# The last dense block of a decoder-layer kernel finished in quarters of 256 columns instead of halves of 512

## The chip, the cores and the metric

The kernel runs on one core of a Trainium2 chip, as one launch. The metric is the device time of that launch in microseconds (us), the median of several executions; lower is better.

## The reference

One decoder layer on 512 tokens of width 1024: a mixer (sliding-window attention beside gated linear attention), then a retrieval of experts, then a final norm. Only the end matters here:

```
def peer_ffn(h, wq, subkeys, u, v):
    ...                                   # 16 experts per head and token, gates by softmax
        hid = jax.nn.gelu(jnp.einsum('tkd,td->tk', ub, xb), approximate=False) * gb
        return jnp.einsum('tk,tkd->td', hid, vb)
...
        x = x + gate2 * peer_ffn(h2, peer_wq[l], peer_subkeys[l], peer_u[l], peer_v[l])
    return rms_norm(x, final_norm_w)      # x * rsqrt(mean(x*x) + 1e-6) * w
```

There are 16384 experts, so `u` and `v` are 16384 x 1024 each, in float32.

## The kernel before

The 512 tokens are four blocks of 128. Blocks 0, 1, 2 (`DENSE`, called `n0`, `n1`, `n2` at the end) are computed densely: every expert's weight for every token stands in a matrix `A` that is mostly zeros, and the block's result is A^T times `v`. Block 3 (`GB`) gathers its experts' rows instead and is finished earlier.

The dense product runs over 128 chunks of 128 experts. Each operand is split into a high and a low part, and `mm3` issues three matmuls per product (lines 98, 99 and 100: high by high, high by low, low by high). The results gather in six accumulators of PSUM, `acc[2*i + q]` for block i and half q of the 1024 columns. Each accumulator has 128 x 512 float32 and fills one bank of PSUM. So `acc0` and `acc1` belong to block 0, `acc2` and `acc3` to block 1, `acc4` and `acc5` to block 2.

For most chunks all six accumulators are served in turn. The last four chunks (`LAST = 4`, the list `last`) are kept back and done block by block, so that block 0 is complete first: 24 matmuls into `acc0` and `acc1`, then 12 into `acc2`, 12 into `acc3`, 12 into `acc4` and 12 into `acc5`. These are the last matmuls of the program.

Then each block is closed. `close_half(n, src, q)` multiplies a half of the accumulator by the gate (L2041, VectorE), adds the residual (L2042, VectorE), and squares the result on ScalarE with a running sum (L2043, followed by a read of the sum, ACTIVATION_READ_ACCUMULATOR). `root(n)` adds the two half sums (L2048), scales them (L2049), and takes the reciprocal root through Ln and Exp on ScalarE (L2050, L2051). `refine(n)` is a correcting step on VectorE (L2057, L2058). `weighted(n, q, w)` multiplies a half by the norm's weights before the root is known (L2061, VectorE), and `scaled` finishes it with the root on ScalarE (L2064) and stores it from ScalarE's queue. `last_half` does both multiplications in one VectorE instruction (L2073) and stores from SP's queue.

Each engine executes its instructions in the order in which they stand in the program. Between engines, the framework places semaphore waits: an instruction waits for what wrote its operands. The two halves of block 2 are closed around the root of block 1, as the end of the printed code shows.

Of the kernel before, what the change touches and what calls it, by code (L numbers as in the profile page):

```python
# [7 lines left out]
F32 = mybir.dt.float32  # L8
# [4 lines left out]
AF = mybir.ActivationFunctionType  # L13
OP = mybir.AluOpType
# [3 lines left out]
P = 128  # L18
D = 1024
# [3 lines left out]
EPS = 1e-6  # L23
# [4 lines left out]
DENSE = (0, 1, 2)  # L28
# [41 lines left out]
def peer_block_kernel(ctx: ExitStack, tc: tile.TileContext, a: dict, out: bass.AP):  # L70
    nc = tc.nc
# [25 lines left out]
    def mm3(acc, lh, ll, rh, rl, start, stop):  # L97
        nc.tensor.matmul(acc, lh, rh, start=start, stop=False)  # L98
        nc.tensor.matmul(acc, lh, rl, start=False, stop=False)  # L99
        return nc.tensor.matmul(acc, ll, rh, start=False, stop=stop)  # L100
# [112 lines left out]
    for L in LW:  # L213
        m = 64 >> L
# [1666 lines left out]
    dn = ctx.enter_context(tc.tile_pool(name="dn", bufs=1, side="right", reuse_waits="tile"))  # L1881
    pacc = ctx.enter_context(tc.tile_pool(name="pacc", bufs=1, space=PSUM, side="right", reuse_waits="tile"))
    acc = [pacc.tile([P, 512], F32, name=f"acc{i}") for i in range(2 * len(DENSE))]
# [131 lines left out]
    def v_matmuls(parts, blocks=range(len(DENSE)), qs=(0, 1)):  # L2015
        for c, Ah, Al, vh, vl in parts:
            for i in blocks:
                for q in qs:
                    mm3(acc[2 * i + q], Ah[:, i * P:(i + 1) * P], Al[:, i * P:(i + 1) * P],
                        vh[:, q * 512:(q + 1) * 512], vl[:, q * 512:(q + 1) * 512], c == 0, c == P - 1)  # L2020
# [8 lines left out]
    def half(t, q):  # L2029
        return t[:, q * 512:(q + 1) * 512]  # L2030

    gate2b = h2n
    fin = {}
# [5 lines left out]
    def close_half(n, src, q):  # L2039
        y, xr, ss = fin[n][:3]  # L2040
        nc.vector.tensor_tensor(half(y, q), src, half(gate2b, q), OP.mult)  # L2041
        nc.vector.tensor_tensor(half(y, q), half(y, q), half(xr, q), OP.add)  # L2042
        nc.scalar.activation(half(xr, q), half(y, q), AF.Square, accum_out=ss[:, q:q + 1])  # L2043

    def root(n):
        ss = fin[n][2]
        m, r = ss[:, 2:3], ss[:, 3:4]
        nc.vector.tensor_tensor(ss[:, 0:1], ss[:, 0:1], ss[:, 1:2], OP.add)  # L2048
        nc.vector.tensor_scalar(m, ss[:, 0:1], -0.5 / D, -0.5 * EPS, op0=OP.mult, op1=OP.add)  # L2049
        nc.scalar.activation(r, m, AF.Ln, scale=-2.0)  # L2050
        nc.scalar.activation(r, r, AF.Exp, scale=-0.5)  # L2051
        fin[n] += [m, r]

    def refine(n):
        m, r = fin[n][3:5]
        t = fin[n][2][:, 4:5]
        nc.vector.scalar_tensor_tensor(t, r, r, m, op0=OP.mult, op1=OP.mult)  # L2057
        nc.vector.scalar_tensor_tensor(r, t, 1.5, r, op0=OP.add, op1=OP.mult)  # L2058

    def weighted(n, q, w):  # L2060
        nc.vector.tensor_tensor(half(w, q), half(fin[n][0], q), half(fin["w"], q), OP.mult)  # L2061

    def scaled(n, q, w):
        nc.scalar.activation(half(w, q), half(w, q), AF.Copy, scale=fin[n][4])  # L2064
        store(n, q, w, nc.scalar)

    def store(n, q, t, eng=None):
        (eng or nc.sync).dma_start(out[n * P:(n + 1) * P, q * 512:(q + 1) * 512], half(t, q))

    def last_half(n, qs=(1,)):  # L2070
        y, r = fin[n][0], fin[n][4]
        for q in qs:
            nc.vector.scalar_tensor_tensor(half(y, q), half(y, q), r, half(fin["w"], q), op0=OP.mult, op1=OP.mult)  # L2073
            store(n, q, y)
# [38 lines left out]
    for i in range(end):  # L2113
        k, c = xs[i]
# [16 lines left out]
    last = [part for i in range(end, len(xs)) for part in ready.pop(i)]  # L2131
    v_matmuls(last[:3], (0,))
    v_matmuls(last[3:], (0,))
    for b in DENSE[1:]:
        for q in range(2):
            v_matmuls(last, (b,), (q,))

    dn.tile([P, 32], F32, name="gap")
    n0, n1, n2 = DENSE
# [12 lines left out]
    close_half(n1, acc[3], 1)  # L2152
    weighted(n1, 0, w1)
    root(n1)
    close_half(n2, acc[4], 0)
    refine(n1)
    last_half(n1)
    scaled(n1, 0, w1)
    close_half(n2, acc[5], 1)
    weighted(n2, 0, w2)  # L2160
    root(n2)
    weighted(n2, 1, w2)
    refine(n2)
    scaled(n2, 0, w2)
# [64 lines left out]
```

## Time and profile before

| what | value |
|---|---|
| median of 3 runs | 1419.93 us (1419.32 to 1423.29) |
| the profiled execution | 1420.04 us, of which its span is 1418.1 us |
| busy: TensorE matmuls, VectorE, ScalarE | 98%, 89%, 46% of the span |
| last matmul starts | 1409.82 us after the span's start |
| last VectorE and ScalarE instructions start | 1414.00 us |

PE is TensorE, PEld its weight loads, DVE VectorE, ACT ScalarE, POOL GpSimd, SP SyncE; ACTq and SPq are those engines' queues of DMA issues. In a timeline row the columns are the start in us from the span's start, the duration in us, the engine, the line, the operation with its tiles (output, arrow, inputs; numbers of buffers are left out), its sizes, and how many instructions the row holds. In brackets stands how long the engine had been idle and what released it. A following instruction of the same engine may start a little before the former one's end, since the engines are pipelined.

### The profile page before, as it was taken

The numbers are of one execution on the slowest core, as the hardware profiler recorded it, in microseconds if no ns is written. First come the engines' busy times: TensorE is split into PE (matmuls) and PEld (weight loads), VectorE is DVE, ScalarE is ACT, GpSimd is POOL, SyncE is SP. The second block draws the span as 40 slices with busy tenths as digits, with TensorE's granted clock in tenths as the row PEclk, the third lists the DMA queues.
The fourth block names the chain that finished last, engine by engine and source line by source line (L and its number), as shares of the span: only waits on it lengthen the run. The fifth ranks groups of instructions, "written<-read, shape, count | busy, mean of one in ns | idle before, by whom it ended". The sixth has DMA issues, their size and how long they took to land.

```text
span 1418.1 us, 23363 instructions
## 1 busy us (share of the span) xinstructions
PE 1394.5 (98%) x8838; PEld 1226.5 (86%) x8838; DVE 1258.4 (89%) x2312; ACT 658.9 (46%) x1116; POOL 604.0 (43%) x397
## 2 busy tenths in 40 slices
PE   8999999999999999999989999999999999999997
PEld 5777788988999999999978888888888888888886
DVE  7768888679899999998969899989898998998996
ACT  4458565533534567667844333333333333333333
POOL 1000000344616443232045766767677776555520
PEclk9999999999999999999999999999999999999999
DMA  9621567422559989899889999999999999999972
GB/s 356 258 93 58 165 221 246 133 98 70 193 193 413 339 320 378 320 349 345 296 326 414 412 412 413 411 412 411 402 405 387 403 378 412 402 412 405 411 260 75
DMA packets 128305, 439.88 MB, mean 310 GB/s; under 512 B 11936, under 2 KB 48832, under 8 KB 107840
## 3 DMA queue, kind: packets, MB, share of 16 engines
q1 hardware_dynamic: 69600, 252.73, 47.2%
q0 software_dynamic: 47136, 171.99, 31.0%
q10 hardware_dynamic: 11456, 13.67, 2.7%
q8 instruction: 69, 1.13, 0.3%
q14 instruction: 44, 0.36, 0.1%
HBM read 395.78 MB, written 42.47 MB: 309 GB/s over the span
## 4 chain that ended last, share of the span: by engine, by line
PE 80%; DVE 7%; issue 6%; POOL 3%; DMA 2%; ACT 2%; SPq 0%; POOLq 0%; DVEq 0%; ACTq 0%
PE acc L98 12%; PE acc L100 12%; PE acc L99 12%; PE ph L98 8%; PE ph L100 8%; PE ph L99 8%; POOL spr L1631 3%; PE pq L99 2%; PE pq L98 2%; PE pq L100 2%; PE pg L1552 2%; PE pw L98 1%; PE pw L100 1%; PE pw L99 1%; PE pj L509 1%
## 5 line engine op out<-in xcount | busy, mean ns | idle before, releaser
L98 PE MATMUL ph<-h2Th,his 128*128 128x320 f32 x1024 | 319.5, 312 | 2.8 <-ACT his L1995 1.9
L100 PE MATMUL ph<-h2Th,los 128*128 128x320 f32 x1024 | 316.0, 310 | 2.5 <-DVE los L2002 1.8
L99 PE MATMUL ph<-h2Tl,his 128*128 128x320 f32 x1024 | 316.0, 309 | 0.0
L1687 POOL DMA_INDIRECT gu<-in_u_dram,ix_u x128 | 212.1, 1657 | 151.1 <-DVE gu L1697 82.4
L1722 POOL DMA_INDIRECT gv<-in_vP_dram,ix_v x128 | 210.2, 1642 | 111.9 <-DVE gacc L1727 87.0
L98 PEld LDWEIGHTS ph<-h2Th,his 128*128 128x128 f32 x1024 | 192.7, 188 | 4.7 <-ACT his L1995 2.1
L100 PEld LDWEIGHTS ph<-h2Th,los 128*128 128x128 f32 x1024 | 192.4, 188 | 3.4 <-DVE los L2002 2.0
L99 PEld LDWEIGHTS ph<-h2Tl,his 128*128 128x128 f32 x1024 | 192.7, 188 | 0.8
L1631 POOL DMA_INDIRECT spr<-in_u_dram,spix x64 | 104.0, 1625 | 174.0 <-DVE spr L1637 130.1
L98 PE MATMUL acc<-his,Ah 128*128 128x512 f32 x432 | 168.0, 389 | 0.0
L99 PE MATMUL acc<-los,Ah 128*128 128x512 f32 x432 | 168.0, 389 | 0.0
L100 PE MATMUL acc<-his,Al 128*128 128x512 f32 x432 | 168.0, 389 | 0.0
L1727 DVE SCALAR_TENSOR_TENSOR gacc<-gv,hg,gacc 128x1024 f32<-128x1024 f32 x127 | 162.5, 1279 | 3.3 <-DMA gv<-in_vP_dram,ix_v 3.1
L1697 DVE SCALAR_TENSOR_TENSOR gu<-gu,h2n 128x1024 f32<-128x1024 f32 x128 | 155.4, 1218 | 4.3 <-DMA gu<-in_u_dram,ix_u 4.3
L98 PE MATMUL acc<-hi,Ah 128*128 128x512 f32 x336 | 131.3, 391 | 0.0
L100 PE MATMUL acc<-hi,Al 128*128 128x512 f32 x336 | 131.1, 390 | 0.0
L99 PE MATMUL acc<-lo,Ah 128*128 128x512 f32 x336 | 130.7, 389 | 0.0
L1998 ACT ACTIVATE Ah<-gr 128x768 fp32r<-128x768 f32 x64 | 53.5, 836 | 140.0 <-PE acc L99 128.4
L91 ACT ACTIVATE his<-u 128x1024 fp32r<-128x1024 f32 x86 | 90.4, 1054 | 25.8 <-PE ph L99 13.5
L98 PEld LDWEIGHTS acc<-his,Ah 128*128 128x128 f32 x432 | 81.1, 188 | 16.9
L100 PEld LDWEIGHTS acc<-his,Al 128*128 128x128 f32 x432 | 81.1, 188 | 16.8
L99 PEld LDWEIGHTS acc<-los,Ah 128*128 128x128 f32 x432 | 81.1, 188 | 16.8
(712 smaller groups left out, 2883.1 us busy)
## 6 DMA issues: line engine op xcount, KB each, us to landing
u<-in_uT_dram SPq DMA_DIRECT2D x43, 1024.0 KB
gr<-Gd SPq DMA_DIRECT2D x15, 1536.0 KB
Gd<-gs SPq DMA_DIRECT2D x10, 2048.0 KB
gsp<-ge ACTq DMA_DIRECT2D x40, 320.0 KB
wa<-in_w_ada_dram SPq DMA_DIRECT2D x12, 1024.0 KB
wq<-in_wq_dram SPq DMA_DIRECT2D x8, 1024.0 KB
gp<-gsp SPq DMA_DIRECT2D x22, 320.0 KB
gp<-gsp SPq DMA_DIRECT2D x36, 160.0 KB
```

Source lines behind the costliest of these rows:

```text
L91: nc.scalar.activation(hi, src, AF.Copy)
L98: nc.tensor.matmul(acc, lh, rh, start=start, stop=False)
L99: nc.tensor.matmul(acc, lh, rl, start=False, stop=False)
L100: return nc.tensor.matmul(acc, ll, rh, start=False, stop=stop)
L509: return [(lambda p=p, w=w, r=r, s=s, e=e: nc.tensor.matmul(p, w, r[:, k, :], start=s, stop=e)) for p, w, r, s, e in jobs]
L1552: nc.tensor.matmul(pt[:, i, :], o12[:, g, 0, :, r], o2[:, g, m, :, r], start=(m == 0), stop=(m == 2))
L1631: nc.gpsimd.indirect_dma_start(out=sp[m], out_offset=None, in_=a["u"], in_offset=bass.IndirectOffsetOnAxis(ap=sp["ix", i][:, j:j + 1], axi ...
L1687: nc.gpsimd.indirect_dma_start(out=ur, out_offset=None, in_=a["u"], in_offset=bass.IndirectOffsetOnAxis(ap=ix_u[:, s:s + 1], axis=0))
L1697: nc.vector.scalar_tensor_tensor(ur, ur, 1.0, h2n, op0=OP.mult, op1=OP.mult, accum_out=hid[:, s:s + 1])
L1722: nc.gpsimd.indirect_dma_start(out=vr, out_offset=None, in_=a["vP"], in_offset=bass.IndirectOffsetOnAxis(ap=ix_v[:, s:s + 1], axis=0))
L1727: nc.vector.scalar_tensor_tensor(gacc, vr, hg[:, s:s + 1], gacc, op0=OP.mult, op1=OP.add)
L1998: nc.scalar.activation(grp(Ah), A, AF.Copy)
```

## The change

Block 2's last matmuls are issued in quarters: 256 columns of `acc4`, 256 of `acc5`, then the other 256 of `acc4`, and of `acc5`. Blocks 0 and 1 are as before. The block is closed with four calls of `close_quarter` (L2165 to L2167) in the same order. Three of the four partial sums are added and scaled (L2177 to L2179) ahead of the last quarter's close; the fourth goes in with one instruction (L2182) that replaces the two of `root`.

```diff
-    for b in DENSE[1:]:
+    for q in range(2):
+        v_matmuls(last, (1,), (q,))
+    for c0 in (0, 256):
         for q in range(2):
-            v_matmuls(last, (b,), (q,))
+            for c, Ah, Al, vh, vl in last:
+                cs = slice(q * 512 + c0, q * 512 + c0 + 256)
+                mm3(acc[4 + q][:, c0:c0 + 256], Ah[:, 2 * P:], Al[:, 2 * P:], vh[:, cs], vl[:, cs], c == 0, c0 == 256 and c == P - 1)
...
-    close_half(n2, acc[4], 0)
+    y2, xr2 = fin[n2][:2]
+    parts = dn.tile([P, 4], F32, name="parts")
+
+    def close_quarter(i):
+        c0, q = divmod(i, 2)
+        cs = slice(q * 512 + c0 * 256, q * 512 + c0 * 256 + 256)
+        nc.vector.tensor_tensor(y2[:, cs], acc[4 + q][:, c0 * 256:c0 * 256 + 256], gate2b[:, cs], OP.mult)
+        nc.vector.tensor_tensor(y2[:, cs], y2[:, cs], xr2[:, cs], OP.add)
+        nc.scalar.activation(xr2[:, cs], y2[:, cs], AF.Square, accum_out=parts[:, i:i + 1])
+
+    close_quarter(0)
     refine(n1)
+    close_quarter(1)
     last_half(n1)
     scaled(n1, 0, w1)
-    close_half(n2, acc[5], 1)
+    close_quarter(2)
+    ss = fin[n2][2]
+    m, r = ss[:, 2:3], ss[:, 3:4]
+    nc.vector.tensor_tensor(ss[:, 0:1], parts[:, 0:1], parts[:, 1:2], OP.add)
+    nc.vector.tensor_tensor(ss[:, 0:1], ss[:, 0:1], parts[:, 2:3], OP.add)
+    nc.vector.tensor_scalar(ss[:, 0:1], ss[:, 0:1], -0.5 / D, -0.5 * EPS, op0=OP.mult, op1=OP.add)
+    close_quarter(3)
     weighted(n2, 0, w2)
-    root(n2)
+    nc.vector.scalar_tensor_tensor(m, parts[:, 3:4], -0.5 / D, ss[:, 0:1], op0=OP.mult, op1=OP.add)
+    nc.scalar.activation(r, m, AF.Ln, scale=-2.0)
+    nc.scalar.activation(r, r, AF.Exp, scale=-0.5)
+    fin[n2] += [m, r]
     weighted(n2, 1, w2)
     refine(n2)
     scaled(n2, 0, w2)
```

The built programs of before and of the change are the same up to block 2's last matmuls, except for buffer numbers. Three places differ. In the rows below, numbers in names tell buffers apart (`acc4_8485` is `acc[4]`), and brackets name the semaphores that an instruction waits for: PE_49 counts TensorE's progress, Activation_49 ScalarE's, DVE_49 VectorE's own, and DMAHW and DMASW transfers.

First, TensorE where it passes from one accumulator of block 2 to the next. Before, there is one such place, from `acc4` to `acc5`:

```order
L98 MATMUL acc4_8485<-his_2005,Ah126_13415 128x512
L99 MATMUL acc4_8485<-los_2006,Ah126_13415 128x512
L100 MATMUL acc4_8485<-his_2005,Al126_13416 128x512
L98 MATMUL acc5_8486<-hi2_8493,Ah124_13357 128x512
L99 MATMUL acc5_8486<-lo2_8494,Ah124_13357 128x512
L100 MATMUL acc5_8486<-hi2_8493,Al124_13358 128x512
```

Now there are three; this is the second, after 24 of the 48 matmuls:

```order
L98 MATMUL acc5_8486<-his_2005,Ah126_13415 128x256
L99 MATMUL acc5_8486<-los_2006,Ah126_13415 128x256
L100 MATMUL acc5_8486<-his_2005,Al126_13416 128x256
L98 MATMUL acc4_8485<-hi2_8493,Ah124_13357 128x256
L99 MATMUL acc4_8485<-lo2_8494,Ah124_13357 128x256
L100 MATMUL acc4_8485<-hi2_8493,Al124_13358 128x256
```

TensorE returns to `acc4`, for its other 256 columns, after 12 matmuls into `acc5`; no matmul here waits for a semaphore.

Second, VectorE from block 1's scaled sum to the first half of block 2 and block 1's last multiplication. Before:

```order
L2049 TENSOR_SCALAR sm1_13542<-sm1_13542 128x1 [waits DVE_49]
L2041 TENSOR_TENSOR y2_13543<-acc4_8485,h2n_1998 128x512 [waits PE_49]
L2042 TENSOR_TENSOR y2_13543<-y2_13543,xf2_13544 128x512 [waits DMAHW1_49,DVE_49]
L2057 SCALAR_TENSOR_TENSOR sm1_13542<-sm1_13542 128x1 [waits Activation_49]
L2058 SCALAR_TENSOR_TENSOR sm1_13542<-sm1_13542 128x1 [waits DVE_49]
L2073 SCALAR_TENSOR_TENSOR y1_13540<-y1_13540,sm1_13542,fwb_13250 128x512 [waits DVE_49]
```

Now:

```order
L2049 TENSOR_SCALAR sm1_13566<-sm1_13566 128x1 [waits DVE_49]
L2165 TENSOR_TENSOR y2_13567<-acc4_8485,h2n_1998 128x256 [waits PE_49]
L2166 TENSOR_TENSOR y2_13567<-y2_13567,xf2_13568 128x256 [waits DMAHW1_49,DVE_49]
L2057 SCALAR_TENSOR_TENSOR sm1_13566<-sm1_13566 128x1 [waits Activation_49]
L2058 SCALAR_TENSOR_TENSOR sm1_13566<-sm1_13566 128x1 [waits DVE_49]
L2165 TENSOR_TENSOR y2_13567<-acc5_8486,h2n_1998 128x256 [waits PE_49]
L2166 TENSOR_TENSOR y2_13567<-y2_13567,xf2_13568 128x256 [waits DVE_49]
L2073 SCALAR_TENSOR_TENSOR y1_13564<-y1_13564,sm1_13566,fwb_13250 128x512
```

The close of `acc5`'s first quarter, with a wait for TensorE, has moved ahead of block 1's last multiplication (L2073).

Third, VectorE from there to the end. Before:

```order
L2041 TENSOR_TENSOR y2_13543<-acc5_8486,h2n_1998 128x512 [waits PE_49]
L2042 TENSOR_TENSOR y2_13543<-y2_13543,xf2_13544 128x512 [waits DVE_49]
L2061 TENSOR_TENSOR w2_13547<-y2_13543,fwb_13250 128x512 [waits DMAHW7_49,DMAHW0_49]
L2048 TENSOR_TENSOR sm2_13546<-sm2_13546 128x1 [waits Activation_49]
L2049 TENSOR_SCALAR sm2_13546<-sm2_13546 128x1 [waits DVE_49]
L2061 TENSOR_TENSOR w2_13547<-y2_13543,fwb_13250 128x512
```

Now:

```order
L2165 TENSOR_TENSOR y2_13567<-acc4_8485,h2n_1998 128x256
L2166 TENSOR_TENSOR y2_13567<-y2_13567,xf2_13568 128x256 [waits DVE_49]
L2177 TENSOR_TENSOR sm2_13570<-parts_13600 128x1 [waits Activation_49]
L2178 TENSOR_TENSOR sm2_13570<-sm2_13570,parts_13600 128x1 [waits DVE_49,Activation_49]
L2179 TENSOR_SCALAR sm2_13570<-sm2_13570 128x1 [waits DVE_49]
L2165 TENSOR_TENSOR y2_13567<-acc5_8486,h2n_1998 128x256
L2166 TENSOR_TENSOR y2_13567<-y2_13567,xf2_13568 128x256 [waits DVE_49]
L2061 TENSOR_TENSOR w2_13571<-y2_13567,fwb_13250 128x512 [waits DMAHW7_49,DMAHW0_49]
L2182 SCALAR_TENSOR_TENSOR sm2_13570<-parts_13600,sm2_13570 128x1 [waits Activation_49]
L2061 TENSOR_TENSOR w2_13571<-y2_13567,fwb_13250 128x512 [waits DVE_49]
```

The sum with the third quarter's part (L2178) waits for ScalarE and stands ahead of the last quarter's close. The reads of the third and fourth quarters (the first and sixth rows) wait for no semaphore of TensorE. ScalarE's order is: two squares, block 1's scaling (L2064) with its store, the other two squares, Ln, Exp; before it was one square, the scaling with its store, the other square, Ln, Exp.

## The prediction

> **What bounds the kernel now.** I read the page's busy times and chain first, then the busy time in stretches of the tail, then the timeline of each engine there.
>
> ```profile
> span 1418.1 us, 23363 instructions
> PE 1394.5 (98%) x8838; PEld 1226.5 (86%) x8838; DVE 1258.4 (89%) x2312; ACT 658.9 (46%) x1116; POOL 604.0 (43%) x397
> PE 80%; DVE 7%; issue 6%; POOL 3%; DMA 2%; ACT 2%; SPq 0%; POOLq 0%; DVEq 0%; ACTq 0%
> 1404.26:1414.48 10.22, 5.95 (x27) 4.59 (x25) 9.53 (x21) 4.48 (x14) 0.00 (x0) 1.00 0.28 103
> 1414.48:1418.10 3.62, 0.00 (x0) 0.00 (x0) 0.00 (x1) 0.24 (x1) 0.00 (x0) 0.61 0.39 145
> ```
>
> The kernel as a whole hangs on TensorE, but the change touches the last 14 us only, and there the limit is another. In the fourth row (stretch; its length, then busy us of PE, PEld, DVE, ACT, POOL; clock, DMA share, GB/s) VectorE is busy for 9.53 of 10.22 us, TensorE for 5.95. After 1414.48 only stores remain.
>
> VectorE's timeline (start, duration):
>
> ```profile
> 1407.99 0.15 DVE L2049 TENSOR_SCALAR sm<-sm 128x1 f32<-128x1 f32 x1
> 1408.06 0.68 DVE L2041 TENSOR_TENSOR y<-acc,h2n 128x512 f32<-128x512 f32 x1
> 1408.77 0.69 DVE L2042 TENSOR_TENSOR y<-y,xf 128x512 f32<-128x512 f32 x1
> 1409.38 0.21 DVE L2057 SCALAR_TENSOR_TENSOR sm<-sm 128x1 f32<-128x1 f32 x1
> 1409.63 0.16 DVE L2058 SCALAR_TENSOR_TENSOR sm<-sm 128x1 f32<-128x1 f32 x1
> 1409.83 0.75 DVE L2073 SCALAR_TENSOR_TENSOR y<-y,sm,fwb 128x512 f32<-128x512 f32 x1
> 1410.49 0.68 DVE L2041 TENSOR_TENSOR y<-acc,h2n 128x512 f32<-128x512 f32 x1
> 1411.21 0.69 DVE L2042 TENSOR_TENSOR y<-y,xf 128x512 f32<-128x512 f32 x1
> 1411.82 0.68 DVE L2061 TENSOR_TENSOR w<-y,fwb 128x512 f32<-128x512 f32 x1
> 1412.69 0.16 DVE L2048 TENSOR_TENSOR sm<-sm 128x1 f32<-128x1 f32 x1 [0.19 <-ACT xf L2043]
> 1412.88 0.15 DVE L2049 TENSOR_SCALAR sm<-sm 128x1 f32<-128x1 f32 x1
> 1412.95 0.68 DVE L2061 TENSOR_TENSOR w<-y,fwb 128x512 f32<-128x512 f32 x1
> 1413.56 0.21 DVE L2057 SCALAR_TENSOR_TENSOR sm<-sm 128x1 f32<-128x1 f32 x1
> ```
>
> From these rows I take the steps from start to start. An instruction that needs the result of the one before starts 0.03 us after its end (1408.06 to 1408.77 is 0.71). One that does not starts 0.08 before it (1408.77 to 1409.38 is 0.61). Both reads of block 2's accumulators (1408.06, 1410.49) follow the previous VectorE instruction without idle time, so here VectorE is late and not TensorE:
>
> ```profile
> 1398.26 0.39 PE L100 MATMUL acc<-his,Al 128*128 128x512 f32 x1
> 1398.69 0.69 DVE L2041 TENSOR_TENSOR y<-acc,h2n 128x512 f32<-128x512 f32 x1 [0.22 <-PE acc L100]
> 1404.61 0.39 PE L98 MATMUL acc<-hi,Ah 128*128 128x512 f32 x1
> 1409.82 0.39 PE L100 MATMUL acc<-his,Al 128*128 128x512 f32 x1
> ```
>
> The first two rows are `acc0`: its last matmul ends at 1398.65 and its reader starts 0.04 later, the price of one wait. The other two are the first and last of block 2's 24 matmuls: 23 steps in 5.21 us, 0.2265 each, ending at 1410.21. The `acc5` read could start at 1410.25 and starts at 1410.49.
>
> ScalarE's timeline:
>
> ```profile
> 1409.50 0.63 ACT L2043 ACTIVATE xf<-y 128x512 f32<-128x512 f32 x1 [0.89 <-DVE y L2042]
> 1410.04 0.18 ACT L2043 ACTIVATION_READ_ACCUMULATOR xf<-y 128x1 f32 x1
> 1410.13 0.71 ACT L2064 ACTIVATE w<-w,sm 128x512 f32<-128x512 f32 x1
> 1410.87 0.36 ACTq L2068 DMA_DIRECT2D out_dram<-w  x1
> 1411.94 0.63 ACT L2043 ACTIVATE xf<-y 128x512 f32<-128x512 f32 x1 [1.10 <-DVE y L2042]
> 1412.47 0.19 ACT L2043 ACTIVATION_READ_ACCUMULATOR xf<-y 128x1 f32 x1
> 1413.07 0.20 ACT L2050 ACTIVATE sm<-sm 128x1 f32<-128x1 f32 x1 [0.41 <-DVE sm L2049]
> 1413.31 0.20 ACT L2051 ACTIVATE sm<-sm 128x1 f32<-128x1 f32 x1
> ```
>
> The end is a chain: close of `acc5`, square, sum, Ln at 1413.07, Exp, two corrections, last scaling, store. What the change does to the time is how far it moves Ln.
>
> **Prices of the new shapes.**
>
> ```profile
> 271.82 0.28 PE L98 MATMUL pq<-h2Th,his 128*128 128x256 f32 x1
> 274.06 0.28 PE L99 MATMUL pq<-h2Tl,his 128*128 128x256 f32 x1
> L99 PEld LDWEIGHTS pq<-h2Tl,his x160: 187/188/192, 244.0 to 348.7; 128*128 128x128 f32 x160
> L363 DVE TENSOR_TENSOR Eg<-Eg,gq 128x256 f32<-128x256 f32 x7 | 2.9, 420 | 2.3 <-ACT Eg L356 2.3
> L1154 ACT ACTIVATE qh__2572<-pq 128x256 f32<-128x256 f32 x4 | 1.3, 374 | 0.0
> L1381 ACT ACTIVATE qsc<-pq 128x512 f32<-128x512 f32 x12 | 7.1, 590 | 17.1 <-PE pq L100 17.1
> ```
>
> - Matmuls of 256 columns: the first two rows are 19 steps apart, 2.24 us, so 0.118 each, 0.28 long. The weight loads take 0.188 (third row) but overlap one another. 48 steps of 0.118 are 5.66 us against 24 of 0.2265, 5.44: TensorE ends 0.23 us later, at 1404.61 + 47 x 0.118 + 0.28 = 1410.44.
> - VectorE at 256 columns: 0.42 (L363) against 0.69 at 512. Half the columns save only 0.27: a pair of closing instructions at 512 steps 0.71 + 0.61 = 1.32, at 256 0.45 + 0.34 = 0.79. Four quarters cost 3.16 against 2.64 for two halves.
> - ScalarE: 0.59 at 512, 0.37 at 256 (L1381, L1154), 0.22 less. So the square is 0.41 and the step from square to sum is 0.75 - 0.22 = 0.53.
>
> **What the quarters wait for.** Before, each half's read waits for the last matmul of its own bank. In the changed program the reads of the first two quarters wait for TensorE and those of the third and fourth do not. Yet the third quarter's matmuls come after the first's. So the first wait must already cover them: the program counts TensorE's progress at the 36th and 48th of the 48 matmuls alone. The first quarter's read waits for all of `acc4`, the second's for all of `acc5`, which is the end of TensorE's work. The alternation of banks then makes `acc4` complete later, not earlier: with the 36th matmul, at 1404.61 + 35 x 0.118 + 0.28 = 1409.02, where before it was with the 12th of 24, 1404.61 + 11 x 0.2265 + 0.39 = 1407.49.
>
> No row of before reads one half of a bank while the other is written, so the trace cannot tell whether the chip would allow it. The Trainium skill, "PSUM — Partial Sum Buffer", section "PSUM bank collisions raise a hardware error", says that a read of a bank that TensorE is writing collides even at other columns, and that waits must be set by bank and not by address. By that rule the sum is the one below; by a wait per column range it would be the first rival's.
>
> **The sum.** Starts in us; before from the rows above, after by the steps above:
>
> | step | before | after | why |
> |---|---|---|---|
> | read of `acc4` | 1408.06 | 1409.06 | waits for 1409.02, + 0.04; VectorE idle 1.00 |
> | second instruction, then corrections of block 1 | 1408.77, 1409.38, 1409.63 | 1409.51, 1409.85, 1410.10 | + 0.45, 0.34, 0.25 |
> | read of `acc5`, first quarter | none | 1410.48 | VectorE free at 1410.17; waits for 1410.44, + 0.04 |
> | its second instruction | none | 1410.93 | + 0.45 |
> | L2073 of block 1 | 1409.83 | 1411.27 | + 0.34 |
> | third quarter | none | 1411.93, 1412.38 | + 0.66 (1409.83 to 1410.49), + 0.45 |
> | its square on ScalarE | none | 1412.90 | see below |
> | sum of three (L2178, L2179) | none | 1413.43, 1413.62 | + 0.53, + 0.19 (1412.69 to 1412.88) |
> | last read of `acc5` | 1410.49 | 1413.69 | + 0.07 (1412.88 to 1412.95) |
> | its second instruction | 1411.21 | 1414.14 | + 0.45 |
> | last square | 1411.94 | 1414.60 | + 0.46 (0.73 less 0.27) |
> | L2182, before L2048 | 1412.69 | 1415.13 | + 0.53 |
> | Ln | 1413.07 | 1415.38 | + 0.25 (L2057 to L2058), before 0.38 |
>
> The third square needs its input (1412.38 + 0.46 = 1412.84) and a free ScalarE. That has the second square at 1411.39, block 1's scaling at 1411.80 (0.63 later, less 0.22), the store's issue at 1412.54 (1410.13 to 1410.87), until 1412.90. I take 1412.90; 1412.84 if the issue held nothing up. While L2178 waits, VectorE stands idle from about 1412.9 to 1413.43, and the last quarter's read is queued behind it. L2177 costs nothing: that idle time covers it.
>
> Ln moves by 2.31. Behind it, `weighted` of the second half (0.68) starts at 1415.26, VectorE is free at 1415.87, and Exp's result lets L2057 start at the same time; before, both also met at 1413.56. So the end moves by 2.31 too. The stores at the end stay: block 1's two are issued about 2 us later, as are block 2's.
>
> Sum: 1420.04 + 2.31 = 1422.35 for an execution like the profiled one, which lies 0.1 above the median; against the median 1422.2. I predict 1422.3. In parts, the path gains 0.9 behind the last read (2.58 us from there to Ln before, 1.69 now), and loses 3.2 ahead of it (1410.49 to 1413.69).
>
> Bounds of the unknown costs. VectorE at 256 columns from PSUM lies between half of 0.68 (six of them on the path, -0.5) and no saving at all (+1.6, and +0.2 for the squares); L363 with 0.42 is the nearest. The matmul step lies between half of 0.2265 (-0.2) and one weight load, 0.188 (+3.3); the row has 0.118. That is 1421.6 to 1424.1 with the matmul row taken as it is.
>
> **Rivals.**
>
> 1. The quarters do what they say: each read waits for its own 12 matmuls. The first quarter ends at 1406.19, the second at 1407.60, and VectorE waits for neither. Then the reads come at 1408.06, 1409.17 and 1410.62, the third square at 1411.59 behind block 1's scaling and its store (second square 1410.08, + 0.41, + 0.74, + 0.36), the last read at 1412.38, Ln at 1414.07: +1.0, 1421.0. The missing waits of the third and fourth reads speak against it. 3 in 100.
> 2. The tail hangs on TensorE alone: VectorE keeps up, L2178 never holds it, and the last read starts 0.04 after the last matmul, 1410.48. Ln then comes at 1412.17, -0.9: 1419.1. That VectorE was busy for 9.53 of 10.22 us speaks against it, and that the change gives it more work. 3 in 100.
> 3. The other side: weight loads pace the narrower matmuls. At 0.188 per step the last one ends at 1404.61 + 47 x 0.188 + 0.28 = 1413.73, 3.3 later than I have it, and every later step with it: 1425.6. It is slower by more than 0.3% from a step of 0.16 on (47 x 0.042 = 1.95 on top of 2.31). The 192 matmuls of `pq` with the same loads run at 0.118. 4 in 100.
> 4. VectorE's narrow instructions save nothing, the upper bound above: 1424.1. 8 in 100; L363 speaks against it.
>
> **How the numbers follow.** My forecast has the remaining 82 in 100. Runs of before lie between 1419.32 and 1423.29, so a median can be off by about 1 us beside the cost. 1420.2 to 1424.2 takes in the forecast with that, the first and the fourth rival, and leaves out the second and the third. About 0.3% (4.3 us) is what a measurement of this kernel tells from no change; 2.3 us lies inside. Slower by over 0.3%, 0.09: the third rival with 0.04, and 0.05 for a median that comes out high by 2 us in my own case or by chance in the fourth. Faster by over 0.3%: no case reaches 1415.7, so 0.02 for what I have not thought of. The same: 0.89.
>
> **What would show it.** Right: 48 matmuls of 256 columns at 0.118, the last ending 0.2 later; about 1.0 us of idle VectorE ahead of the first L2165 and about 0.3 ahead of the second, both released by PE; about 0.5 ahead of L2178, released by ScalarE's square; L2182 about 2.4 after where L2048 stood; the end of the span about 5.0 us after Ln, as before (1418.10 less 1413.07). Wrong: a first L2165 that follows L2049 without idle time (rival 1), a last read within 0.1 of the last matmul's end (rival 2), matmul steps over 0.16 (rival 3), L2165 and L2166 of 0.6 or more (rival 4). The prediction fails if anything before 1404 moves, since I take all of it as unchanged.

## The result, and the profile after

The changed kernel takes 1431.87 us, against 1420.26 us for six runs of the kernel before on the same chip: 1.0081 times as long, with a 95% interval of 1.0068 to 1.0094. Its median is that of six executions, of which one took 4294.00 us at a granted clock of 0.319 and is left out of the ratio (as is one of the kernel before in the first four experiments, 1618.94 us); the median of the other five is 1430.90. The prediction was 1422.3. Of some 11 us, it had foreseen 2.3.

The page of the changed kernel, first its span, the busy times and the shares of the chain:

```profile
span 1430.9 us, 23421 instructions
PE 1405.5 (98%) x8862; PEld 1228.2 (86%) x8862; DVE 1259.3 (88%) x2318; ACT 659.3 (46%) x1120; POOL 613.0 (43%) x397
PE 75%; issue 10%; POOL 5%; DVE 5%; DMA 2%; ACT 2%; SPq 0%; POOLq 0%; ACTq 0%; DVEq 0%
```

The profiled execution took 1432.84 us. Its span is 12.8 us longer than before's 1418.1. TensorE is busy for 11.0 us more (1394.5 before) with 24 matmuls more, and the 24 matmuls cannot be that. So the first thing to do is to cut the span at the first matmul of block 2, which starts at 1404.61 before and at 1415.02 after: 10.4 us of the 12.8 have arisen ahead of it, in code that the change does not touch.

The busy times in stretches show where. The rows hold the stretch, its length, the busy us of PE, PEld, DVE, ACT and POOL with the counts of instructions, then the clock, the DMA share and GB/s. First before, then after, both from about the 5400th matmul to the first of block 2:

```profile
719.20:1404.60 685.40, 680.47 (x3418) 589.59 (x3416) 612.87 (x649) 239.94 (x235) 418.40 (x254) 1.00 0.97 386
```

```profile
720.20:1415.00 694.80, 689.88 (x3417) 590.15 (x3415) 613.22 (x649) 239.81 (x235) 424.13 (x254) 1.00 0.96 381
```

The dense stretch is 9.4 us longer, and TensorE is busy for 9.4 us more, with the same number of matmuls but one at the same granted clock of 1.00. VectorE and ScalarE do the same work in the same time. So the matmuls themselves have become slower. The first 719 us are 1.0 longer; in the other kernels shown here they end anywhere between 716.6 and 721.2, and at 724.6 in that of the fourth experiment, so nothing is read from that.

Grouped by line and form, with the moving operand named (count | busy us, mean ns of one), before:

```profile
L98 PE MATMUL acc<-his,Ah 128*128 128x512 f32 x432 | 168.0, 389 | 0.0
L98 PE MATMUL acc<-hi,Ah 128*128 128x512 f32 x336 | 131.3, 391 | 0.0
```

and after:

```profile
L98 PE MATMUL acc<-his,Ah 128*128 128x512 f32 x428 | 169.2, 395 | 0.0
L100 PE MATMUL acc<-his,Al 128*128 128x512 f32 x428 | 169.2, 395 | 0.0
L99 PE MATMUL acc<-los,Ah 128*128 128x512 f32 x428 | 169.0, 395 | 0.0
L98 PE MATMUL acc<-hi,Ah 128*128 128x512 f32 x332 | 129.6, 390 | 0.0
```

The dense product has two kinds of chunks, by where the split rows of `v` (the moving operand, the first name behind the arrow) stand: `his` and `los`, or `hi` and `lo`. Only the first kind has changed, from 389 to 395 ns. The duration of one matmul contains the overlap with the next, so the step from one start to the next is what counts. TensorE's timeline, in the middle of such a chunk, after:

```profile
1299.97 0.40 PE L98 MATMUL acc<-his,Ah 128*128 128x512 f32 x1
1301.37 0.40 PE L98 MATMUL acc<-his,Ah 128*128 128x512 f32 x1
```

Six steps take 1.40 us, 233.3 ns each; before they took 226.6. The means over all of them are 233.8, 232.9 and 233.5 ns for lines 98, 99 and 100 after, against 226.8, 226.5 and 226.6 before. That is 20.3 ns for each triple of matmuls, and 428 triples make 8.7 of the 9.4 us. Added up one by one, the steps of this kind take 8.6 us more. The other 0.8 lies in a few steps of the `ph` matmuls; the second experiment, which has the addresses of before, has 0.6 of it too. The chunks on `hi` and `lo` stay at 227 to 228.

What the change has done to these matmuls is to move their operands. `parts`, the new tile of 16 bytes per partition, takes 32 bytes in the pool `dn`. It is the last tile that the program places there, but the pool's upper end is fixed: `parts` stands at 217024, where the last tile of before stood (`sm2`), and every tile placed ahead of it lies 32 bytes lower. In the built programs the addresses are (bytes within a partition):

```
            before           after
his         83936            83936
los         100320           100320
Ah          154848, 157920   154816, 157888
Al          160992, 164064   160960, 164032
hi, lo      179680, 187872   179648, 187840
```

The weights `Ah` and `Al` have moved against `his` and `los`, which lie in another pool; `hi` and `lo` have moved along with the weights. Before, `Ah` and `Al` lay a multiple of 256 bytes behind `his` (154848 less 83936 is 277 x 256); after, they lie 32 bytes short of one. This fits the groups that got slower, and it is the theory that the runs below test.

The tail behaves as predicted. VectorE's timeline of after, with the first and last matmul of block 2 and the 36th, whose end the first read awaits:

```profile
1415.02 0.28 PE L98 MATMUL acc<-hi,Ah 128*128 128x256 f32 x1
1419.18 0.28 PE L100 MATMUL acc<-his,Al 128*128 128x256 f32 x1
1420.61 0.28 PE L100 MATMUL acc<-his,Al 128*128 128x256 f32 x1
```

```profile
1418.23 0.15 DVE L2049 TENSOR_SCALAR sm<-sm 128x1 f32<-128x1 f32 x1
1419.50 0.42 DVE L2165 TENSOR_TENSOR y<-acc,h2n 128x256 f32<-128x256 f32 x1 [1.11 <-PE acc L100]
...
1420.92 0.42 DVE L2165 TENSOR_TENSOR y<-acc,h2n 128x256 f32<-128x256 f32 x1 [0.22 <-PE acc L100]
1421.38 0.43 DVE L2166 TENSOR_TENSOR y<-y,xf 128x256 f32<-128x256 f32 x1
1421.72 0.75 DVE L2073 SCALAR_TENSOR_TENSOR y<-y,sm,fwb 128x512 f32<-128x512 f32 x1
1422.39 0.42 DVE L2165 TENSOR_TENSOR y<-acc,h2n 128x256 f32<-128x256 f32 x1
...
1423.94 0.16 DVE L2178 TENSOR_TENSOR sm<-sm,parts 128x1 f32<-128x1 f32 x1 [0.61 <-ACT xf L2167]
...
1424.21 0.41 DVE L2165 TENSOR_TENSOR y<-acc,h2n 128x256 f32<-128x256 f32 x1
...
1425.65 0.16 DVE L2182 SCALAR_TENSOR_TENSOR sm<-parts,sm 128x1 f32<-128x1 f32 x1
```

ScalarE's, from block 1's scaling to Ln:

```profile
1422.26 0.71 ACT L2064 ACTIVATE w<-w,sm 128x512 f32<-128x512 f32 x1
1422.99 0.36 ACTq L2068 DMA_DIRECT2D out_dram<-w  x1
1423.40 0.42 ACT L2167 ACTIVATE xf<-y 128x256 f32<-128x256 f32 x1 [0.43 <-DVE sm L2177]
1425.85 0.20 ACT L2183 ACTIVATE sm<-sm 128x1 f32<-128x1 f32 x1 [0.23 <-DVE sm L2182]
```

The two reads that wait for TensorE, the sum that waits for the third square, and the last read that is queued behind the sum are all there. From block 2's first matmul to Ln it is 10.83 us, where before it was 8.46 (1413.07 less 1404.61), and to the end of the span 15.88 instead of 13.49.

### The profile page after: what moved, and what is told of

The parts are those of the page before. It is cut to its first block, busy times and chain, and to the rows that moved or that the text cites. A ratio compares the mean times of both kernels' runs of the same rounds, so it can differ in the third digit from the quotient of the medians.

```text
span 1430.9 us, 23421 instructions
## 1 busy us (share of the span) xinstructions
PE 1405.5 (98%) x8862; PEld 1228.2 (86%) x8862; DVE 1259.3 (88%) x2318; ACT 659.3 (46%) x1120; POOL 613.0 (43%) x397
## 4 chain that ended last, share of the span: by engine, by line
PE 75%; issue 10%; POOL 5%; DVE 5%; DMA 2%; ACT 2%; SPq 0%; POOLq 0%; ACTq 0%; DVEq 0%
PE acc L98 12%; PE acc L100 12%; PE acc L99 12%; POOL spr L1631 5%; PE ph L100 5%; PE ph L98 5%; PE ph L99 5%; PE pq L99 2%; PE pq L98 2%; PE pq L100 2%; DMA spr<-in_u_dram,spix 1%; PE pg L1552 1%; PE pn L98 1%; PE pn L100 1%; PE pn L99 1%
## 5 line engine op out<-in xcount | busy, mean ns | idle before, releaser
L1687 POOL DMA_INDIRECT gu<-in_u_dram,ix_u x128 | 217.6, 1700 | 148.8 <-DVE gu L1697 83.7
L1722 POOL DMA_INDIRECT gv<-in_vP_dram,ix_v x128 | 213.2, 1666 | 113.3 <-DVE gacc L1727 90.4
L98 PE MATMUL acc<-his,Ah 128*128 128x512 f32 (+1 forms) x436 | 171.5, 393 | 0.0
L100 PE MATMUL acc<-his,Al 128*128 128x512 f32 (+1 forms) x436 | 171.4, 393 | 0.0
L99 PE MATMUL acc<-los,Ah 128*128 128x512 f32 (+1 forms) x436 | 171.2, 393 | 0.0
L98 PE MATMUL acc<-hi,Ah 128*128 128x512 f32 (+1 forms) x340 | 131.8, 388 | 0.0
L100 PE MATMUL acc<-hi,Al 128*128 128x512 f32 (+1 forms) x340 | 131.8, 388 | 0.0
L99 PE MATMUL acc<-lo,Ah 128*128 128x512 f32 (+1 forms) x340 | 131.6, 387 | 0.0
```

The lines of the kernel that those rows point to most:

```text
L1687: nc.gpsimd.indirect_dma_start(out=ur, out_offset=None, in_=a["u"], in_offset=bass.IndirectOffsetOnAxis(ap=ix_u[:, s:s + 1], axis=0))
L1722: nc.gpsimd.indirect_dma_start(out=vr, out_offset=None, in_=a["vP"], in_offset=bass.IndirectOffsetOnAxis(ap=ix_v[:, s:s + 1], axis=0))
```

## The experiments

Each run is compared with runs of the kernel before on the same chip. The kernels differ by some lines in number; line numbers are each kernel's own. The "dense stretch" is the time from the 5400th matmul to block 2's first, in the run's profile: 685.4 us before, 694.8 after. The "distance" is the address of the weights less that of the moving operand, in bytes, and modulo 256 where that is said.

### The addresses alone, without the change

```diff
+    dn.tile([P, 4], F32, name="pad")
```

This is the kernel before with a tile that nobody uses, in the same pool as `parts`, a little ahead of it (in front of the tiles `sm0` to `sm2` instead of behind them). The distance is that of the changed kernel, 32 bytes less than before; the tail is that of before.

> The kernel before with one unused tile of 4 float32 per partition, put where the change puts its tile of partial sums, and nothing else. It moves the weights A and the third operand pair (hi2, lo2) down by 32 bytes per partition in SBUF; the pair his, los stays. Theory A (the 10 us ahead of the tail come from the addresses of matmul operands): the 512-column matmuls on his and los step at 0.233 us instead of 0.227, those on hi2 and lo2 stay at 0.227, and the time is 8 to 10 us above before, 1428 to 1431. Rival B (they come from the changed instructions at the end): 1420, no change.

It took 1429.16 us against 1420.22, 1.0070 times as long (1.0048 to 1.0091). The dense stretch is 694.0 us, and the steps of the three lines on `his` and `los` are 233.6, 233.0 and 233.6 ns. The group of line 98:

```profile
L98 PE MATMUL acc<-his,Ah 128*128 128x512 f32 x432 | 170.8, 395 | 0.0
L98 PE MATMUL acc<-hi,Ah 128*128 128x512 f32 x336 | 131.2, 390 | 0.0
```

An unused tile of 32 bytes costs 8.9 us (6.8 to 12.9 by the interval). The rest of the change is not needed for it. The profiled execution is the fastest of the four: its dense stretch is 8.6 us longer than before's, but its span only 5.9, since the part ahead of that stretch ends at 716.6 instead of 719.2.

### The change alone, with the addresses of before

```diff
-    dn.tile([P, 32], F32, name="gap")
+    dn.tile([P, 24], F32, name="gap")
```

`gap` is an unused tile of the pool `dn` that stood there before. Cut by 32 bytes, it makes room for `parts`, and every other tile lies where it lay before, except the tiles `sm0` to `sm2`, which lie 32 bytes lower.

> The changed kernel with the unused tile named gap cut by 32 bytes per partition, so that the weights and the operand pairs lie where they lay before. Theory A: steps of 0.227 everywhere, and only the cost of the tail is left, 2.3 us: 1422 to 1423.5. Rival B: as the changed kernel, 1430 to 1432.

It took 1422.31 us against 1420.22, 1.0016 (1.0002 to 1.0029). The dense stretch is back at 686.0, the steps at 226.8, 226.8 and 226.4, and the group at its old duration:

```profile
L98 PE MATMUL acc<-his,Ah 128*128 128x512 f32 x428 | 166.5, 389 | 0.0
```

Its tail is that of the changed kernel. What the change itself costs is 2.1 us of measured time (0.3 to 4.1), and this kernel lies on the predicted 1422.3. The two runs together split the loss: about 9 us come from the addresses, about 2 from the quarters.

### Twice the shift

```diff
+    dn.tile([P, 16], F32, name="pad")
```

The kernel before with 64 bytes of padding instead of 32, to see whether any shift costs the same, or whether a period of 64 bytes brings the fast step back.

> The kernel before with an unused tile of 16 float32 (64 bytes per partition) at the same place, so that the weights move by 64 bytes against his and los. Theory A1 (what counts is the distance between moving operand and weights modulo 64 bytes): 1420, steps of 0.227. Theory A2 (any other distance than the tuned one, modulo 128 bytes or more): steps of 0.23 or more on his and los, 1428 or more.

It took 1423.28 us, 1.0029 (1.0019 to 1.0040), with a dense stretch of 688.4. Neither expectation fits: the three lines now differ, with steps of 232.0, 226.5 and 229.3 ns.

```profile
L98 PE MATMUL acc<-his,Ah 128*128 128x512 f32 x432 | 170.5, 395 | 0.0
L100 PE MATMUL acc<-his,Al 128*128 128x512 f32 x432 | 169.6, 393 | 0.0
L99 PE MATMUL acc<-los,Ah 128*128 128x512 f32 x432 | 168.1, 389 | 0.0
```

A period of 64 bytes is ruled out, and so is a loss that grows with the shift.

### Both operands moved, in opposite directions

```diff
+    dn.tile([P, 4], F32, name="pad")
...
+        hl.tile([P, 8], F32, name="padl")
```

The weights lie 32 bytes lower, as in the first experiment, and `his` and `los` 32 bytes higher. The absolute address of the weights is that of the first experiment, the distance that of the third.

> The kernel before with 32 bytes in the weights' pool and 32 bytes ahead of his and los: the weights move down by 32 and his and los up by 32, so that both start at multiples of 64 bytes and their distance changes by 64. Theory A1 (distance modulo 64): the dense matmuls step at 0.227, but his and los are also the weights of the 320-column matmuls, whose moving operand stays, so those would get slower from 0.147 if the same holds for them. Theory A3 (what counts is that his and los, or the weights, do not start at a multiple of 64): the dense matmuls step at 0.233 as in the change.

It took 1422.95 us, 1.0021 (1.0009 to 1.0033). The steps are 232.0, 226.5 and 229.4: neither theory's, but those of the third experiment and not of the first. So the distance decides, and not where the weights stand by themselves. In the 96 triples of 512 columns into `pq` the roles are exchanged: `h2Th` and `h2Tl` are the moving operands and lie where they lay, `his` and `los` are the weights and have moved. Their distance goes from 192 to 224 modulo 256, as the dense product's does between the third experiment and the first, and their steps go from 230.0, 231.1 and 227.9 to 232.9, 233.1 and 233.3. The many `ph` matmuls of 320 columns, whose distance changes in the same way, have a median step of 147 ns, as before.

### The distance by itself

This kernel computes nothing of the reference. It runs batches of 36 matmuls (12 triples of the same kind as `mm3`) that differ in the distance and nothing else, in a few batches also in the start of both operands or in the columns:

```
for name, d, s, n in BATCHES:          # d: distance in bytes, s: start of both, n: columns
    ow, om = (d + s) // 4, s // 4
    wh, wl = w[:, ow:ow + P], w[:, ow + 1024:ow + 1024 + P]
    mh, ml = m[:, om:om + n], m[:, om + 1024:om + 1024 + n]
    ...                                # 12 times: wh by mh, wh by ml, wl by mh
```

At `d` = 0 the two operands lie a multiple of 256 bytes apart.

> Matmuls alone, of which nothing of the reference is computed: 36 per batch with the pattern of the dense product (high by high, high by low, low by high), each batch with another start of the weights and the moving operand in SBUF; the batch's name says the distance of the weights from a multiple of 128 bytes behind the moving operand. Theory A1 (distance modulo 128 sets the step): 0.2265 us at 512 columns for zero, onetwentyeight, twofiftysix and fivetwelve and for the four batches where both are moved alike, 0.2335 for thirtytwo and ninetysix, a pattern of 0.2265 to 0.232 with a mean near 0.229 for sixtyfour. Theory A3 (absolute start): the batches moved alike differ from zero. For 256 columns 0.118 to 0.119 at each distance. What distances of 4 to 24 do is open.

TensorE's timeline, the first matmul of a batch and the last, for the distances 0 and 32:

```profile
25.86 0.39 PE L48 MATMUL zero<-moving,weights 128*128 128x512 f32 x1
...
33.79 0.40 PE L50 MATMUL zero<-moving,weights 128*128 128x512 f32 x1
...
67.37 0.40 PE L48 MATMUL thirtytwo<-moving,weights 128*128 128x512 f32 x1
...
75.54 0.40 PE L50 MATMUL thirtytwo<-moving,weights 128*128 128x512 f32 x1
```

35 steps take 7.93 us, 226.6 ns each, or 8.17, 233.4 each. In the same way all batches of 512 columns:

```
distance in bytes   step in ns
0                   226.7   (repeated at the end: 227.5)
4, 8, 16, 24        232.5, 230.5, 233.3, 230.0
32                  233.4   (repeated: 233.2)
40, 48, 56, 60      233.3, 233.3, 233.3, 230.4
64                  233.1   (repeated: 233.4)
72, 80, 96, 112     233.3, 232.0, 234.2, 233.3
128                 233.5
192                 228.9   (232, 226 and 229 by line)
256, 512            227.0, 226.7
0, both operands started 4, 16, 32, 64 bytes later: 237.6, 231.2, 227.2, 227.4
```

The same by the groups, with the 320-column batches:

```profile
L48 PE MATMUL onetwentyeight<-moving,weights 128*128 128x512 f32 x12 | 4.7, 395 | 0.0
L48 PE MATMUL twofiftysix<-moving,weights 128*128 128x512 f32 x12 | 4.7, 389 | 0.0
L48 PE MATMUL fifthzero<-moving,weights 128*128 128x320 f32 x12 | 3.7, 309 | 0.0
L48 PE MATMUL fifththirtytwo<-moving,weights 128*128 128x320 f32 x12 | 3.7, 309 | 0.0
```

The fast step comes back at 256 and 512 bytes, not at 128, where it had been expected. The distance 64 was expected at 229 and came out at 233; the pattern of the third and fourth experiments, 232, 226 and 229, belongs to 192, which is their distance once it is counted modulo 256 (64 bytes less). The changed kernel's own distance, 224, is not among the batches. At distances that are no multiple of 32 the weights' start is none either, so these batches do not tell the two apart; and of the batches with both operands moved alike, those moved by 32 and 64 stay at 227, while those moved by 4 and 16 do not. Hardly a transfer runs beside these batches (a DMA share of 0.00, against 0.97 in the dense stretch), so transfers are not needed for the effect. No distance is faster than 0. Narrower matmuls show nothing of it: at 256 columns the steps are 119.8, 118.3 and 117.8 for the distances 0, 32 and 64, at 320 columns 146.7, 146.5 and 146.7.

### A shift of 128 and of 256 bytes in the kernel

The small kernel says that 128 bytes of padding must cost what 32 cost, and 256 nothing. The kernel before with

```diff
+    dn.tile([P, 32], F32, name="pad")
```

> The kernel before with an unused tile of 128 bytes per partition in the weights' pool: the weights and hi2, lo2 move by 128 bytes against his and los. Theory A4 (the distance counts modulo 256 bytes, as the batches of matmuls alone say): steps of about 0.2335 on his and los, 8 to 9 us more, 1428 to 1431. Theory A1 (modulo 128): 0.2265 and 1420.

took 1426.01 us against 1421.06, 1.0044 (1.0027 to 1.0061). The steps are 233.1, 233.0 and 233.5, as a period of 256 bytes has it, and the dense stretch is 692.8, 7.5 longer than before's.

```profile
L98 PE MATMUL acc<-his,Ah 128*128 128x512 f32 x432 | 170.5, 395 | 0.0
```

The time is only 4.9 longer, though 8 to 9 were expected. In the profiled execution the span is 5.8 longer (1423.9). There the steps on `his` and `los` take 8.3 us more, those on `hi` and `lo` 0.8 less, and the dense stretch begins at 717.6 instead of 719.2, which lies within what that part differs by among the kernels here. Why `hi` and `lo` gain is open, and one profile does not show whether the medians come about in the same way.

And the changed kernel with `gap` enlarged by 224 bytes, so that together with `parts` the weights and `hi2`, `lo2` lie 256 bytes lower:

```diff
-    dn.tile([P, 32], F32, name="gap")
+    dn.tile([P, 88], F32, name="gap")
```

> The changed kernel with the unused tile named gap longer by 224 bytes per partition, so that with its own 32 the weights move by 256 bytes in all against his and los. Theory A4 (modulo 256): steps of 0.2265 and only the tail's 2.4 us are left, 1422 to 1423.5. If each absolute address other than the tuned one costs: steps of 0.23 and more, 1428 or more.

took 1422.62 us, 1.0012 (1.0000 to 1.0023). The dense stretch is 685.9, the steps 226.8, 226.7 and 226.4, and the group is that of the second experiment:

```profile
L98 PE MATMUL acc<-his,Ah 128*128 128x512 f32 x428 | 166.5, 389 | 0.0
```

A tile of 32 bytes costs 9 us; eight times as much room leaves the dense stretch as it was, to 0.5 us.

### The sum behind the last quarter's close

The other runs are about the tail's 2.4 us, and both are built on the second experiment, so that the addresses are those of before. They are read from the tail alone, as times from block 2's first matmul. Each was run once, at 1420.49 and 1420.55 us against 1419.43 for a run of the kernel before on the same chip, and single runs cannot tell these times apart.

```diff
     nc.vector.tensor_tensor(ss[:, 0:1], parts[:, 0:1], parts[:, 1:2], OP.add)
+    close_quarter(3)
     nc.vector.tensor_tensor(ss[:, 0:1], ss[:, 0:1], parts[:, 2:3], OP.add)
...
-    close_quarter(3)
```

> The change at the addresses of before (as e2), with the addition of the third partial sum and its scaling moved behind the last quarter's close. If the wait of that addition for ScalarE's square holds the last quarter back, as the prediction has it, the last read of acc5 starts about 1.0 us earlier relative to block 2's first matmul than in e2, and the end about 0.75 earlier. If the wait is covered by something else, nothing moves. In time: 0.75 us of 1422, seen in the profile alone.

The second experiment's rows, the sum and the last read:

```profile
1403.63 0.28 PE L98 MATMUL acc<-hi,Ah 128*128 128x256 f32 x1
...
1412.59 0.16 DVE L2178 TENSOR_TENSOR sm<-sm,parts 128x1 f32<-128x1 f32 x1 [0.60 <-ACT xf L2167]
...
1412.86 0.41 DVE L2165 TENSOR_TENSOR y<-acc,h2n 128x256 f32<-128x256 f32 x1
```

and those of this kernel, where the read goes ahead of the sum:

```profile
1403.36 0.28 PE L98 MATMUL acc<-hi,Ah 128*128 128x256 f32 x1
...
1411.57 0.15 DVE L2177 TENSOR_TENSOR sm<-parts 128x1 f32<-128x1 f32 x1
1411.63 0.42 DVE L2165 TENSOR_TENSOR y<-acc,h2n 128x256 f32<-128x256 f32 x1
...
1412.43 0.15 DVE L2179 TENSOR_TENSOR sm<-sm,parts 128x1 f32<-128x1 f32 x1
```

The last read starts 8.27 us after block 2's first matmul instead of 9.23, right behind L2177. The sum of three (in this kernel L2179) comes 0.80 after it and waits for nothing. The span's end comes at 15.17 instead of 15.91, 0.74 earlier, where 0.75 was expected. It is still 1.7 later than before's 13.49.

### TensorE's halves, with the quarters' close

```diff
-    for c0 in (0, 256):
+    for b in DENSE[1:]:
         for q in range(2):
...
+            v_matmuls(last, (b,), (q,))
```

Block 2's matmuls are again 24 of 512 columns, `acc4` first; VectorE still closes in quarters.

> The change at the addresses of before (as e2), with TensorE's part undone: block 2's matmuls in halves of 512 columns as before, the closes in quarters as changed. If reads wait for whole banks, the first read of acc4 follows block 1's scaled sum without idle time (about 1.0 us earlier than in e2 relative to block 2's first matmul), and the read of acc5's first quarter still waits for the last matmul, which ends 0.23 earlier; the end moves by about 0.2. If the first quarter's read had waited for its own 12 matmuls, it would not start earlier here than in e2.

```profile
1403.02 0.39 PE L98 MATMUL acc<-hi,Ah 128*128 128x512 f32 x1
...
1406.39 0.16 DVE L2049 TENSOR_SCALAR sm<-sm 128x1 f32<-128x1 f32 x1
1406.46 0.41 DVE L2161 TENSOR_TENSOR y<-acc,h2n 128x256 f32<-128x256 f32 x1
...
1408.66 0.42 DVE L2161 TENSOR_TENSOR y<-acc,h2n 128x256 f32<-128x256 f32 x1 [1.00 <-PE acc L100]
```

and the second experiment's first read, whose first matmul started at 1403.63:

```profile
1408.14 0.42 DVE L2165 TENSOR_TENSOR y<-acc,h2n 128x256 f32<-128x256 f32 x1 [0.98 <-PE acc L100]
```

The first read comes 3.44 after block 2's first matmul, 1.07 earlier than in the second experiment, and follows L2049 without idle time. But the second read, of `acc5`, still waits for the last matmul, now with 1.00 of idle time ahead of it. The end comes at 15.60, 0.31 earlier; 0.2 was expected. So issuing the matmuls in alternating quarters costs 0.31 in this chain, its later end included; the larger part of the 1.07 is lost again at the next wait. The two edits together were not tried. No whole kernel here is faster than the kernel before.

## Why the prediction was wrong, and where it was right

**The step that failed** is the assumption in the last sentence: "The prediction fails if anything before 1404 moves, since I take all of it as unchanged." The change adds the tile `parts`, and the prediction gave it no price at all: it counted instructions, waits and queues, and left out where the tiles lie. That the two programs are the same up to block 2's last matmuls, as is said ahead of the prediction, holds for their instructions and not for their addresses. The missing term is +8.9 us in measured time (the unused tile alone), 8.6 by the steps on `his` and `los`, both in the changed kernel and with the unused tile alone. The other 0.8 of the 9.4 us in the changed kernel's dense stretch, in steps of `ph`, is not explained. The range could not hold the time, since none of its cases touched that stretch.

**The tail's sum** was right. In us from block 2's first matmul:

| step | predicted | measured |
|---|---|---|
| read of `acc4` | 4.45 | 4.48 |
| last matmul's end | 5.83 | 5.87 |
| read of `acc5`, first quarter | 5.87 | 5.90 |
| L2073 of block 1 | 6.66 | 6.70 |
| third quarter's read | 7.32 | 7.37 |
| third square | 8.29 | 8.38 |
| sum of three (L2178) | 8.82 | 8.92 |
| last read | 9.08 | 9.19 |
| L2182 | 10.52 | 10.63 |
| Ln | 10.77 | 10.83 |
| end of the span | 15.80 | 15.88 |

Ln moved by 2.37 us (predicted 2.31), and the end with it. With the addresses of before, the same change measures 1422.31. Two slips in the working change nothing of this: with the matmul row taken as it is, the lower bound is 1421.8 and not 1421.6, and 47 x 0.042 is 1.97 and not 1.95.

**The prices.** 256-column matmuls step at 0.119 (predicted 0.118). VectorE takes 0.42 for 256 columns, read from PSUM or not, so that the narrow instructions do save what the nearest row said, and the fourth rival is out. Idle time ahead of the three waiting instructions was 1.11, 0.22 and 0.61, against 1.0, 0.3 and 0.5.

**What the quarters wait for** was right. The first read starts at 1419.50, 0.04 after the 36th matmul's end (1419.18 + 0.28), not after its own twelfth. The first rival is out, and the run with halves on TensorE shows the same by the 1.07 that the read gains there. This agrees with the Trainium skill, "PSUM — Partial Sum Buffer", section "PSUM bank collisions raise a hardware error", which has waits set by bank; what the chip would do with a read of the other half of a bank in use, no run here shows.

**The second and third rivals.** The last read starts 3.32 us after the last matmul's end (1424.21 less 1420.89) and not 0.04 after it; weight loads do not pace the narrow matmuls, at 0.119 against the 0.16 from which that would have decided.

**That the sum's wait holds up the last read** was right too: moved behind it, the end comes 0.74 earlier.

**Why the distance matters** stays open. Shown is that it decides, with a period of 256 bytes, in matmuls of 512 columns that alternate with weight loads. That the reading of the weights and of the moving operand get in each other's way would fit, and is only argued. The Trainium skill, "TensorE: Matmul & The Clock Gate", section "Step-by-step: what each phase is for", says that TensorE has two independent read ports to SBUF, and that loading the next weights takes no bandwidth from the running matmul. By that rule the distance would change nothing; 226.7 against 233.4 ns between two batches that differ in nothing else says that at 512 columns something does, and the measurement decides.

## What to carry to other kernels

A new tile, however small, can move others in SBUF, and the step of a 512-column matmul can depend on where its two operands lie; so before a change with a tile in it is costed at instructions and waits alone, compare the addresses of the operands of the program's most frequent matmuls before and after. In a kernel of 512-column matmuls, keep the weights a multiple of 256 bytes from the moving operand, and both at multiples of 32, and take the room of new small tiles from padding that is there. To place the tile last is no safeguard: `parts` was the last of its pool and moved the tiles placed ahead of it. When a profile differs in a place that the edit does not touch, look at the groups by form first: here, a group whose duration moved with its count and the granted clock unchanged pointed to the operands and not to the schedule.

## What the hardware showed unexpectedly

- A matmul of 128x512 float32 (`float32r` in the code) with a weight load per matmul steps at 226.7 to 227.5 ns when the distance of its operands is 0, 256 or 512 bytes, and at 230 to 234 at every other distance tried up to 128; at 192 it is 229 on average, 232, 226 and 229 by the place in the triple.
- At 256 and 320 columns the distances 0, 32 and 64 make no such difference (117.8 to 119.8 and 146.5 to 146.7 ns).
- The start counts as well: with the distance 0 but both operands started 4 or 16 bytes later the step is 237.6 or 231.2 ns; at 32 and 64 bytes it is 227.2 and 227.4.
